# Two of four weight sums by adding transfers in the seven-product blocks of an MLP's down projection (Trainium2, one core)

## The chip, the core and the metric

The kernel runs on one core of one Trainium2 chip. Its time is the device time of one execution in microseconds, the median of several runs. Five engines work side by side, each from a queue of its own: PE (matrix products), DVE (element by element), ACT (element by element with a function; here mostly copies that round), POOL (a further element engine, which can also issue transfers) and SP (here transfers alone). Transfers are carried by 16 transfer engines, whichever queue has issued them.

## What is computed

One decoder layer over 256 tokens of width 2048 in float32: a norm, an input projection, two groups of attention heads, an output projection with a residual, and an MLP with a residual and a last norm. The change lies in the MLP's second product.

```python
def reference(x, ...):
    ...
    x = x + mixed @ w_out[l]                                        # (256, 2048) @ (2048, 2048)
    h = rms_norm(x, norm2_g[l])
    x = x + jnp.square(jax.nn.relu(h @ w_mlp_in[l])) @ w_mlp_out[l]  # 2048 -> 8192 -> 2048
    return rms_norm(x, final_norm_g)
```

## The kernel before

*Precision.* Every float32 operand is held as two rounded parts, hi and lo, with hi + lo the operand (lo is the residue after rounding). A product is then three matrix products: hi·hi, hi·lo, lo·hi. For weights, ACT makes hi from the loaded tile (whi from raw) and DVE subtracts to get lo (wlo). This "split" is done for 128 x 1024 weights at a time.

*The MLP.* It runs in four rounds of 2048 hidden units. In a round, 16 tiles of 128 rows by 512 columns form a column block; four column blocks of the up projection ("u") and four of the down projection ("d") follow one another. Weights are loaded in units of 512 rows by 512 columns (1 MB, tile raw, four tiles deep, `[128, 4, 512]`) by SP's queue, and are consumed in steps of two 128-row tiles. A raw tile can be loaded again when all that is read from it has been read; the function `load_more` keeps four units that aren't spent. A unit's last split marks it as spent.

*Seven products.* For seven of the 16 down blocks (d block 0 of the rounds 0 to 2, d block 1 of all rounds) a unit of 512 x 512 weights with its 256 tokens is regarded as a 2 x 2 matrix of blocks, tokens in two halves, rows in two halves (k tiles 0, 1 and 2, 3) and columns in two halves of 256. Instead of eight block products, seven are computed, from sums and differences of the activation blocks (mix_hi, mix_lo; made by `mix_activations`) and of the weight blocks. A unit has four steps: "near" (the lower weight rows as they are), "first" (the upper left block), "odd" (two weight sums) and "even" (two further ones). There are 28 such units. The weight sums are made on DVE: ahead of "near", one operation makes the tile both (128 x 1024) from differences of raw; it is split for "odd"; then two operations of 128 x 512 overwrite both with the sums for "even", and it is split again. With "odd", raw is spent. `drain_seven` adds the seven products, which stand in PSUM, into the residual xs with the right signs and the factor rstd2sq.

*Order.* A list of steps, written out when the program is built, sets the order on PE; "near", "first", "odd", a plain step, "even", then further plain steps. In the up blocks there is one unit to eight plain steps; where down block 1 is mixed with down block 2, a unit and two plain steps alternate, four times in a round (below: the alternating stretch). Splits are written several steps ahead of their products, as far as five rotating whi and wlo buffers allow, so an ACT split waits until PE has finished with an older buffer. Nothing reorders instructions.

Of the kernel before, what the change touches and what calls it, by code (L numbers as in the profile page):

```python
# [11 lines left out]
F32 = mybir.dt.float32  # L12
F32R = mybir.dt.float32r
BF16 = mybir.dt.bfloat16
AF = mybir.ActivationFunctionType
ALU = mybir.AluOpType
# [3 lines left out]
P = 128  # L20
D_MODEL = 2048
SEQ = 256
TB = SEQ // P
# [5 lines left out]
CW = 512  # L29
# [47 lines left out]
def kernel(  # L77
# [18 lines left out]
    nc = tc.nc  # L96
# [11 lines left out]
    few = ctx.enter_context(tc.tile_pool(name="few", bufs=1))  # L108
# [29 lines left out]
    steps = [(ci, s, "") for ci in range(mlp0) for s in range(chunks[ci][6] // 2)]  # L138
# [25 lines left out]
    raws, splits, spent = {}, {}, set()  # L164

    def load(i):
        if i >= len(steps) or steps[i][1] % 2 or (steps[i][0], steps[i][1] // 2) in raws:
            return
        ci, s, _ = steps[i]
        _, _, w, r0, c0, cols, _ = chunks[ci]  # L170
        t = wraw.tile([P, 4, CW + NH], F32, name="raw")
        src = w[r0 + s * 256:r0 + s * 256 + 512, c0:c0 + cols].rearrange("(k p) c -> p k c", p=P)
        raws[ci, s // 2] = t
        if i == 0:
            return t, src
        n = 2 if i == 2 else 4
        for k in range(0, 4, n):
            nc.sync.dma_start(t[:, k:k + n, :cols], src[:, k:k + n])

    def load_more():  # L180
        for ci, unit in units:
            if len(raws) - len(spent) >= 4:
                return
            if (ci, unit) not in raws:
                load(steps.index(next(p for p in steps if p[0] == ci and p[1] // 2 == unit)))
# [3 lines left out]
    def part_tiles(i, size, high, low):  # L189
        if i < mlp_start:  # L190
            pool, names = wsplit, ("whi", "wlo")
        else:
            ring[0] += 1
            pool, names = (late_tiles["ring"], ("whi5", "wlo5")) if ring[0] % 5 == 0 else (wsplit, ("whi", "wlo"))
        return [pool.tile([P, 2 * CW + LINE], F32R, name=n)[:, b:b + size] for n, b in zip(names, (high, low))]

    late_tiles, late_forms, sums_of = {}, ExitStack(), {}

    def halves(t):
        return t.rearrange("p k (f c) -> p f k c", f=2)  # L200

    def split_seven(i):
        ci, s, sub = steps[i]
        t = raws[ci, s // 2][:, :, :CW]
        half = CW // 2
        if sub == "near":
            both = sums_of[ci, s] = late_tiles["pool"].tile([P, 2, CW], F32, name="both")
            nc.vector.tensor_tensor(halves(both), t[:, :, half:].rearrange("p (f k) c -> p f k c", f=2),
                                    halves(t[:, :2]), op=ALU.subtract)
        if sub == "first":  # L210
            hi, lo = (late_tiles["pool"].tile([P, CW + LINE], F32R, name=n)[:, b:b + CW]
                      for n, b in (("fhi", NEAR), ("flo", NEAR)))
            src = t[:, :2, :half]
        else:
            hi, lo = part_tiles(i, 2 * CW, NEAR, NEAR)
            src = t[:, 2:] if sub == "near" else sums_of[ci, s]
        hi, lo = (a.rearrange("p (k c) -> p k c", k=2) for a in (hi, lo))
        splits[i] = (hi, lo)
        nc.scalar.activation(hi, src, AF.Copy)  # L219
        nc.vector.tensor_tensor(lo, src, hi.bitcast(F32), op=ALU.subtract)  # L220
        if sub == "odd":
            a, b = src[:, :, :half], src[:, :, half:]
            nc.vector.tensor_tensor(a, t[:, 2:, half:], a, op=ALU.subtract)
            nc.vector.tensor_tensor(b, t[:, 2:, :half], a, op=ALU.subtract)  # L224
            spent.add((ci, s // 2))

    def split(i, j0=0, n=2):
        if i >= len(steps):
# [46 lines left out]


    raw0, src0 = load(0)
    load_x(0, 2, nc.sync, slice(0, 1))
    load_row(0)
# [6 lines left out]
    load_row(1, nc.scalar)  # L286
    nc.scalar.dma_start(grow[0:16], norm1_g[0].rearrange("(k p) -> k p", p=P))
    load(2)
    for c in range(2, 4):
        load_x(4 * c, 4 * c + 4)  # L290
# [65 lines left out]
    def rsqrt(dst, ssq, n):  # L356

        w = dst.shape[1]
        v = few.tile([P, TB], F32, name="rs_v", bufs=2)[:, :w]
        t = few.tile([P, TB], F32, name="rs_t", bufs=2)[:, :w]  # L360
        nc.vector.tensor_scalar(v, ssq, 1.0 / n, EPS, op0=ALU.mult, op1=ALU.add)
        nc.gpsimd.tensor_tensor(dst, v, half_t[:, :w], op=ALU.pow)
        nc.vector.tensor_tensor(t, dst, dst, op=ALU.mult)
        nc.vector.tensor_tensor(t, t, v, op=ALU.mult)
        nc.vector.tensor_scalar(t, t, -0.5, 1.5, op0=ALU.mult, op1=ALU.add)
        nc.vector.tensor_tensor(dst, dst, t, op=ALU.mult)
# [349 lines left out]
    ssq2s = few.tile([P, TB], F32, name="ssq2s")  # L716
    rstd2 = few.tile([P, TB], F32, name="rstd2")
    rstd2sq = few.tile([P, TB], F32, name="rstd2sq")

    def drain_o(kind, c, ci):  # L720
        acc = accs.pop(ci)
        for t in range(TB):
            xc = xs[:, t, c * CW:(c + 1) * CW]
            nc.vector.scalar_tensor_tensor(xc, acc[t], rstdo[kind][:, t:t + 1], xc, op0=ALU.mult, op1=ALU.add)
            if kind == 1:
                unused = two.tile([P, CW], F32, name="nat")
                nc.scalar.activation(unused, xc, AF.Square, accum_out=ssq2[:, t, c:c + 1])

    def second_norm():
        nc.vector.tensor_reduce(ssq2s, ssq2, axis=mybir.AxisListType.X, op=ALU.add)  # L730
        rsqrt(rstd2, ssq2s, D_MODEL)
        nc.vector.tensor_tensor(rstd2sq, rstd2, rstd2, op=ALU.mult)

    def squares():
        return rows_at(big_hi, BIG_HI), rows_at(big_lo, BIG_LO)
# [19 lines left out]
    def mix_activations(c):  # L755

        a, b = kept[c]
        (a11, a21), (a12, a22) = ((x[:, :, :P], x[:, :, P:]) for x in (a, b))
        nc.vector.tensor_tensor(a22, a21, a22, op=ALU.add)
        nc.vector.tensor_tensor(a21, a11, a21, op=ALU.subtract)  # L760
        nc.vector.tensor_tensor(a11, a22, a11, op=ALU.subtract)  # L761
        nc.vector.tensor_tensor(a12, a12, a11, op=ALU.subtract)

    def split_mixed(c):
# [19 lines left out]
    def drain_seven(r, c, ci, part):  # L784
        one_, two_, three, four = accs[ci]
        half = CW // 2
        left, right = slice(0, half), slice(half, CW)

        def add(t, cs, acc):
            xc = xs[:, t, cs]  # L790
            if len(acc.shape) > 2:
                xc = xc.rearrange("p (f c) -> p f c", f=2)
            nc.vector.scalar_tensor_tensor(xc, acc, rstd2sq[:, t:t + 1], xc, op0=ALU.mult, op1=ALU.add)

        cs = slice(c * CW, (c + 1) * CW)
        rest = three[:, right]
        if part == 0:
            s = late_tiles["ring"].tile([P, 2, half], F32, name="copies")
            late_tiles["copies"] = s
            nc.scalar.activation(s[:, 0], three[:, left], AF.Copy)  # L800
            nc.scalar.activation(s[:, 1], four[:, left], AF.Copy)
            nc.vector.tensor_tensor(rest, rest, s[:, 0], op=ALU.add)
            add(0, cs, one_)
        elif part == 1:
            add(0, cs, three)
            add(0, slice(cs.start + half, cs.stop), two_[:, right])
        elif part == 2:
            nc.vector.tensor_tensor(rest, rest, late_tiles["copies"][:, 1], op=ALU.add)
            add(1, cs, two_)
        else:  # L810
            add(1, cs, rest[:, None, :].to_broadcast([P, 2, half]))
            accs.pop(ci)
        if r == ROUNDS - 1 and part % 2:
            square_and_gain(part // 2, cs, c)

    def square_and_gain(t, cs, n):
        unused = two.tile([P, CW], F32, name="nat")
        nc.scalar.activation(unused[:, :cs.stop - cs.start], xs[:, t, cs], AF.Square, accum_out=ssq3[:, t, n:n + 1])
        if n > 2:
            put_gain(t, cs)  # L820
# [213 lines left out]
```

## Time and profile before

| | |
|---|---|
| median of three runs | 1089.61 us (1089.52 to 1090.16) |
| profiled execution | 1087.94 us, of which 1086.2 us span of the trace |
| busy share of the span | PE 99%, PE's weight loads 93%, DVE 74%, ACT 56%, POOL 3% |
| granted PE clock | 0.997 |
| moved by transfers | 209.26 MB, 193 GB/s |

The span runs from the first instruction to the last; the rest of the execution's time lies around it. A busy share is that of an engine over the whole span. In rows of groups, a name such as wlo<-raw,whi gives the tiles written and read, x28 the count, then the busy time in us, the mean of one in ns, and the engine's idle time ahead of them with what ended it. Rows of the order of time begin with start and duration in us.

### The profile page before, as it was taken

Reading aid. Unit: us, or ns where it says so; the run is one execution under the profiler, and the core shown is the slowest. Engines: PE = TensorE matmul, PEld = TensorE weight load, DVE = VectorE, ACT = ScalarE, POOL = GpSimd, SP = SyncE. Lnnn points to the kernel's source line nnn. Section 1 sums busy time; section 2 is a strip of 40 time slices with the busy share of each in tenths; the row PEclk is TensorE's granted clock in tenths of the full one; section 3 lists DMA queues with packets and bytes.
Section 4 is the critical chain, followed back from the end, with each engine's and each line's share of the span. In section 5 each row is a group of like instructions: output and inputs, shape, how many; then the busy total and the mean of one; then the engine's idle time right before and its main releaser. Section 6 shows DMA issues by size and latency. Waiting matters only on the chain.

```text
span 1086.2 us, 18976 instructions
## 1 busy us (share of the span) xinstructions
PE 1073.9 (99%) x7877; PEld 1007.0 (93%) x7877; DVE 800.3 (74%) x1076; ACT 604.4 (56%) x821; POOL 28.0 (3%) x42
## 2 busy tenths in 40 slices
PE   8999999999999999999999999999999999999996
PEld 7999899998988899998999998899998999999886
DVE  6667756667577666568877788887778886778885
ACT  6555545545454555565546665556665545666561
POOL 0010200000001000000000000000000000000000
PEclk9999999999999999999999999999999999999998
DMA  9764564655545566655675655665656665656552
GB/s 322 237 228 161 157 199 149 194 165 181 199 155 185 164 184 210 193 190 192 203 215 193 203 197 171 208 203 174 204 204 210 187 195 187 195 195 232 193 195 78
DMA packets 105394, 209.26 MB, mean 193 GB/s; under 512 B 3971, under 2 KB 5084, under 8 KB 105180
## 3 DMA queue, kind: packets, MB, share of 16 engines
q1 hardware_dynamic: 104412, 206.59, 58.3%
q8 instruction: 61, 1.00, 0.4%
q0 software_dynamic: 304, 1.06, 0.3%
q10 hardware_dynamic: 592, 0.40, 0.2%
q14 instruction: 25, 0.20, 0.1%
HBM read 205.93 MB, written 2.11 MB: 192 GB/s over the span
## 4 chain that ended last, share of the span: by engine, by line
PE 99%; DMA 0%; DVE 0%; POOL 0%; ACTq 0%; DVEq 0%; issue 0%
PE acc L417 48%; PE acc L401 34%; PE sc L461 7%; PE tr L461 5%; PE tr L350 1%; PE sc L691 1%; PE sc L401 1%; PE sc L647 1%; PE tr L675 0%; DMA xs<-in_x_dram 0%; PE sc L643 0%; PE sc L693 0%; PE sc L637 0%; PE sc L641 0%; DVE xs L859 0%; PE sc L695 0%
## 5 line engine op out<-in xcount | busy, mean ns | idle before, releaser
L254 DVE TENSOR_TENSOR wlo<-raw,whi 128x1024 fp32r<-128x1024 f32 (+2 forms) x327 | 394.0, 1220 | 155.2 <-ACT whi L253 152.9
L253 ACT ACTIVATE whi<-raw 128x1024 fp32r<-128x1024 f32 (+2 forms) x328 | 339.3, 1050 | 223.5 <-PE acc L417 130.4
L417 PE MATMUL acc<-aT_hi,whi 128*128 128x256 f32 x1536 | 425.6, 277 | 0.0
L417 PE MATMUL acc<-aT_hi,wlo 128*128 128x256 f32 x1536 | 424.0, 276 | 0.0
L417 PE MATMUL acc<-aT_lo,whi 128*128 128x256 f32 x1536 | 423.8, 276 | 0.0
L417 PEld LDWEIGHTS acc<-aT_hi,whi 128*128 128x128 f32 x1536 | 288.2, 188 | 1.2 <-issue 0.9
L417 PEld LDWEIGHTS acc<-aT_lo,whi 128*128 128x128 f32 x1536 | 288.2, 188 | 0.3
L417 PEld LDWEIGHTS acc<-aT_hi,wlo 128*128 128x128 f32 x1536 | 288.1, 188 | 0.1
L401 PE MATMUL acc<-whi,big_lo 128*128 128x512 f32 (+1 forms) x414 | 160.8, 388 | 0.0
L401 PE MATMUL acc<-whi,big_hi 128*128 128x512 f32 (+1 forms) x414 | 160.3, 387 | 0.0
L401 PE MATMUL acc<-wlo,big_hi 128*128 128x512 f32 (+1 forms) x414 | 160.0, 386 | 0.0
L401 PEld LDWEIGHTS acc<-wlo,big_hi 128*128 128x128 f32 x414 | 77.8, 188 | 15.9
L401 PEld LDWEIGHTS acc<-whi,big_lo 128*128 128x128 f32 x414 | 77.7, 188 | 15.2
L401 PEld LDWEIGHTS acc<-whi,big_hi 128*128 128x128 f32 x414 | 77.7, 188 | 15.2
L219 ACT ACTIVATE whi<-both 128x1024 fp32r<-128x1024 f32 x56 | 59.7, 1067 | 52.6 <-DVE both L224 24.8
L220 DVE TENSOR_TENSOR wlo<-both,whi 128x1024 fp32r<-128x1024 f32 x56 | 68.3, 1220 | 7.5 <-ACT whi L219 6.5
L337 DVE TENSOR_TENSOR big_lo<-nat,big_hi 128x512 fp32r<-128x512 f32 x32 | 22.2, 693 | 43.7 <-ACT big_hi L336 43.7
L401 PE MATMUL acc<-whi,aT_hi 128*128 128x512 f32 (+1 forms) x144 | 51.7, 359 | 0.0
L401 PE MATMUL acc<-whi,aT_lo 128*128 128x512 f32 (+1 forms) x144 | 51.0, 354 | 0.0
L401 PE MATMUL acc<-wlo,aT_hi 128*128 128x512 f32 (+1 forms) x144 | 51.0, 354 | 0.0
L219 ACT ACTIVATE whi<-raw 128x1024 fp32r<-128x1024 f32 x28 | 29.6, 1058 | 11.8 <-PE acc L401 6.4
L336 ACT ACTIVATE mix_hi<-nat 128x512 fp32r<-128x512 f32 x32 | 18.5, 625 | 29.9 <-DVE nat L761 29.9
(212 smaller groups left out, 1351.2 us busy)
## 6 DMA issues: line engine op xcount, KB each, us to landing
raw<-in_w_mlp_in_dram SPq DMA_DIRECT2D x64, 1024.0 KB, 5.7
raw<-in_w_mlp_out_dram SPq DMA_DIRECT2D x64, 1024.0 KB, 5.1
raw<-in_w_in_dram SPq DMA_DIRECT2D x42, 1024.0 KB, 5.1
raw<-in_w_out_dram SPq DMA_DIRECT2D x16, 1024.0 KB, 5.0
raw<-in_w_in_dram SPq DMA_DIRECT2D x4, 1040.0 KB, 8.5
xs<-in_x_dram SPq DMA_DIRECT2D x3, 512.0 KB, 9.7
raw<-in_w_in_dram SPq DMA_DIRECT2D x2, 512.0 KB, 5.4
big_lo<-rel_d POOLq DMA_DIRECT2D x1, 1024.0 KB, 7.2
```

The lines of the kernel that those rows point to most:

```text
L219: nc.scalar.activation(hi, src, AF.Copy)
L220: nc.vector.tensor_tensor(lo, src, hi.bitcast(F32), op=ALU.subtract)
L253: nc.scalar.activation(hi[:, :, c:c + step], t[:, :, c:c + step], AF.Copy)
L254: nc.vector.tensor_tensor(lo, t, hi.bitcast(F32), op=ALU.subtract)
L336: nc.scalar.activation(hi, src, AF.Copy)
L337: nc.vector.tensor_tensor(lo, src, hi.bitcast(F32), op=ALU.subtract)
L350: nc.tensor.transpose(p[:, j * SEQ + t * P:j * SEQ + (t + 1) * P], xs[:, t, c:c + P], ident)
L401: nc.tensor.matmul(acc, x, part[:, j, cols], start=go and n == 0, stop=end and n == 2, skip_group_check=True)
L417: nc.tensor.matmul(acc, w[:, j, b * P:(b + 1) * P], a[:, kt, :], start=kt == 0 and b % 2 == 0 and n == 0, stop=kt == kts - 1 and n == 2, s ...
L461: nc.tensor.matmul(acc, a[:, k, tokens], w[:, j, n * half:(n + 1) * half], start=fresh and x == 0, stop=s == KT // 2 - 2 and j == 1 and x ...
L647: nc.tensor.matmul(s[:, c0:c1], q[:, a, h, rows], k[:, b, h, keys], start=False, stop=n == 2, skip_group_check=True)
L691: nc.tensor.matmul(y[:, :SEQ], v[:, 0, dims], p[:, m, :SEQ], start=n == 0, stop=False, skip_group_check=True)
```

## The change

Two of the four weight sums of a unit are no longer made by DVE from raw. One is made in place, by a transfer issued on POOL that adds the upper left block of the weights, read again from memory, to the upper right block in raw. The other goes into a new tile third (128 x 2 x 256, two buffers): SP's queue loads the upper right block into it, and POOL's queue adds the lower right block. "odd" is then split from raw's upper right part and from third, in two halves each on ACT and DVE. Two additions on DVE within raw follow, and "even" is split from raw, at once, in a four-dimensional form. With "even", and no longer with "odd", raw is spent. The signs of one block column are turned round: two subtractions become additions among the weights, and on the activations, the drain and its factor (rstd2neg) the signs follow; the last drain is done in two halves of 256 columns instead of one broadcast over 512.

```diff
@@ load
+        if steps[i][2]:
+            half = CW // 2
+            third = sums_of[ci, s] = late_tiles["pool"].tile([P, 2, half], F32, name="third", bufs=2)
+            nc.sync.dma_start(third, src[:, :2, half:])
+            nc.gpsimd.dma_start(t[:, :2, half:CW], src[:, :2, :half], accum_op=ALU.add)
+            nc.gpsimd.dma_start(third, src[:, 2:, half:], accum_op=ALU.add)
@@ split_seven
-        if sub == "near":
-            both = sums_of[ci, s] = late_tiles["pool"].tile([P, 2, CW], F32, name="both")
-            nc.vector.tensor_tensor(halves(both), t[:, :, half:].rearrange("p (f k) c -> p f k c", f=2),
-                                    halves(t[:, :2]), op=ALU.subtract)
...
-            src = t[:, 2:] if sub == "near" else sums_of[ci, s]
+            parts = {"near": [(slice(0, CW), t[:, 2:])],
+                     "odd": [(left, t[:, :2, right]), (right, sums_of.get((ci, s)))],
+                     "even": [(left, t[:, :2, right]), (right, t[:, 2:, right])]}[sub]
...
-        nc.scalar.activation(hi, src, AF.Copy)
-        nc.vector.tensor_tensor(lo, src, hi.bitcast(F32), op=ALU.subtract)
+        if sub == "even":
+            h, l = (a.rearrange("p k (f c) -> p f k c", f=2) for a in (hi, lo))
+            x = t[:, :, right].rearrange("p (f k) c -> p f k c", f=2)
+            nc.scalar.activation(h, x, AF.Copy)
+            nc.vector.tensor_tensor(l, x, h.bitcast(F32), op=ALU.subtract)
+            spent.add((ci, s // 2))
+            return
+        for c, x in parts:
+            nc.scalar.activation(hi[:, :, c], x, AF.Copy)
+            nc.vector.tensor_tensor(lo[:, :, c], x, hi[:, :, c].bitcast(F32), op=ALU.subtract)
         if sub == "odd":
-            a, b = src[:, :, :half], src[:, :, half:]
-            nc.vector.tensor_tensor(a, t[:, 2:, half:], a, op=ALU.subtract)
-            nc.vector.tensor_tensor(b, t[:, 2:, :half], a, op=ALU.subtract)
-            spent.add((ci, s // 2))
+            sums_of.pop((ci, s))
+            first, second = t[:, :2, right], t[:, 2:, right]
+            nc.vector.tensor_tensor(first, first, second, op=ALU.add)
+            nc.vector.tensor_tensor(second, first, t[:, 2:, left], op=ALU.add)
@@ second_norm
+        nc.vector.tensor_scalar(rstd2neg, rstd2sq, -1.0, None, op0=ALU.mult)
@@ mix_activations
-        nc.vector.tensor_tensor(a22, a21, a22, op=ALU.add)
+        nc.vector.tensor_tensor(a22, a21, a22, op=ALU.subtract)
         nc.vector.tensor_tensor(a21, a11, a21, op=ALU.subtract)
-        nc.vector.tensor_tensor(a11, a22, a11, op=ALU.subtract)
+        nc.vector.tensor_tensor(a11, a11, a22, op=ALU.subtract)
@@ drain_seven
-            nc.vector.tensor_tensor(rest, rest, s[:, 0], op=ALU.add)
+            nc.vector.tensor_tensor(rest, rest, s[:, 0], op=ALU.subtract)
...
-            nc.vector.tensor_tensor(rest, rest, late_tiles["copies"][:, 1], op=ALU.add)
+            nc.vector.tensor_tensor(rest, rest, late_tiles["copies"][:, 1], op=ALU.subtract)
...
-            add(1, cs, rest[:, None, :].to_broadcast([P, 2, half]))
+            add(1, slice(cs.start, cs.start + half), rest, rstd2neg)
+            add(1, slice(cs.start + half, cs.stop), rest)
```

On DVE, one period of the alternating stretch reads so before: the difference (both), the splits of "near", "first" and "odd", the two sums for "even", a plain split, "even", a plain split.

```order
L208 TENSOR_TENSOR both<-raw 128x2x2x256
L220 TENSOR_TENSOR wlo<-raw,whi 128x1024
L220 TENSOR_TENSOR flo<-raw,fhi 128x512
L220 TENSOR_TENSOR wlo<-both,whi 128x1024
L223 TENSOR_TENSOR both<-raw,both 128x2x256
L224 TENSOR_TENSOR both<-raw,both 128x2x256
L254 TENSOR_TENSOR wlo<-raw,whi 128x1024
L220 TENSOR_TENSOR wlo<-both,whi 128x1024
```

And the same period on DVE after the change:

```order
L230 TENSOR_TENSOR wlo<-raw,whi 128x1024
L230 TENSOR_TENSOR flo<-raw,fhi 128x512
L230 TENSOR_TENSOR wlo<-raw,whi 128x2x256
L230 TENSOR_TENSOR wlo<-third,whi 128x2x256
L234 TENSOR_TENSOR raw<-raw 128x2x256
L235 TENSOR_TENSOR raw<-raw 128x2x256
L264 TENSOR_TENSOR wlo<-raw,whi 128x1024
L225 TENSOR_TENSOR wlo<-raw,whi 128x2x2x256
```

The first row is gone, the split of "odd" stands in two rows, the sums are written into raw, and raw is read until the last row. On SP's queue the alternating stretch now has a transfer into third behind every unit's load (x2 stands for a unit's load and a plain unit's load):

```order
L182 DMA third<-in_w_mlp_out_dram 128x2x256
L178 DMA raw<-in_w_mlp_out_dram 128x4x512 x2
L182 DMA third<-in_w_mlp_out_dram 128x2x256
L178 DMA raw<-in_w_mlp_out_dram 128x4x512 x2
L182 DMA third<-in_w_mlp_out_dram 128x2x256
```

On POOL's queue, which has nothing between the MLP's start and the last norm before the change, stand two transfers for each unit, 56 in all. The one into raw waits for the unit's load, the one into third for the transfer on SP:

```order
L183 DMA raw<-in_w_mlp_out_dram 128x2x256
L184 DMA third<-in_w_mlp_out_dram 128x2x256
L183 DMA raw<-in_w_mlp_out_dram 128x2x256
L184 DMA third<-in_w_mlp_out_dram 128x2x256
L183 DMA raw<-in_w_mlp_out_dram 128x2x256
```

What moved there is where a sum is waited for: ACT's split of "odd" now waits for these transfers, the splits of "near" and "first" for the unit's load alone. PE's order of products has not moved.

More of the change, by code (lines that the diff above doesn't have):

```diff
@@ L197 @@
     late_tiles, late_forms, sums_of = {}, ExitStack(), {}
-    def halves(t):
-        return t.rearrange("p k (f c) -> p f k c", f=2)
     def split_seven(i):
@@ L205, in split_seven @@
         half = CW // 2
-        if sub == "near":
-            both = sums_of[ci, s] = late_tiles["pool"].tile([P, 2, CW], F32, name="both")
-            nc.vector.tensor_tensor(halves(both), t[:, :, half:].rearrange("p (f k) c -> p f k c", f=2),
-                                    halves(t[:, :2]), op=ALU.subtract)
+        left, right = slice(0, half), slice(half, CW)
         if sub == "first":
@@ L212, in split_seven @@
                       for n, b in (("fhi", NEAR), ("flo", NEAR)))
-            src = t[:, :2, :half]
+            parts = [(slice(0, half), t[:, :2, left])]
         else:
             hi, lo = part_tiles(i, 2 * CW, NEAR, NEAR)
-            src = t[:, 2:] if sub == "near" else sums_of[ci, s]
+            parts = {"near": [(slice(0, CW), t[:, 2:])],
+                     "odd": [(left, t[:, :2, right]), (right, sums_of.get((ci, s)))],
+                     "even": [(left, t[:, :2, right]), (right, t[:, 2:, right])]}[sub]
         hi, lo = (a.rearrange("p (k c) -> p k c", k=2) for a in (hi, lo))
         splits[i] = (hi, lo)
-        nc.scalar.activation(hi, src, AF.Copy)
-        nc.vector.tensor_tensor(lo, src, hi.bitcast(F32), op=ALU.subtract)
+        if sub == "even":
[8 more added lines that the diff above has]
+            nc.vector.tensor_tensor(lo[:, :, c], x, hi[:, :, c].bitcast(F32), op=ALU.subtract)
         if sub == "odd":
-            a, b = src[:, :, :half], src[:, :, half:]
-            nc.vector.tensor_tensor(a, t[:, 2:, half:], a, op=ALU.subtract)
-            nc.vector.tensor_tensor(b, t[:, 2:, :half], a, op=ALU.subtract)
-            spent.add((ci, s // 2))
+            sums_of.pop((ci, s))
+            first, second = t[:, :2, right], t[:, 2:, right]
+            nc.vector.tensor_tensor(first, first, second, op=ALU.add)
+            nc.vector.tensor_tensor(second, first, t[:, 2:, left], op=ALU.add)
     def split(i, j0=0, n=2):
@@ L718 @@
     rstd2sq = few.tile([P, TB], F32, name="rstd2sq")
+    rstd2neg = few.tile([P, TB], F32, name="rstd2neg")
     def drain_o(kind, c, ci):
@@ L787, in drain_seven, with add @@
         left, right = slice(0, half), slice(half, CW)
-        def add(t, cs, acc):
+        def add(t, cs, acc, scale=rstd2sq):
             xc = xs[:, t, cs]
-            if len(acc.shape) > 2:
-                xc = xc.rearrange("p (f c) -> p f c", f=2)
-            nc.vector.scalar_tensor_tensor(xc, acc, rstd2sq[:, t:t + 1], xc, op0=ALU.mult, op1=ALU.add)
+            nc.vector.scalar_tensor_tensor(xc, acc, scale[:, t:t + 1], xc, op0=ALU.mult, op1=ALU.add)
         cs = slice(c * CW, (c + 1) * CW)
```

## The prediction

> **What bounds the kernel now.** I read the page's busy table and its chain of waits first, then windows over the stage that the change touches, then that stage's order of time.
>
> ```profile
> span 1086.2 us, 18976 instructions
> PE 1073.9 (99%) x7877; PEld 1007.0 (93%) x7877; DVE 800.3 (74%) x1076; ACT 604.4 (56%) x821; POOL 28.0 (3%) x42
> PE 99%; DMA 0%; DVE 0%; POOL 0%; ACTq 0%; DVEq 0%; issue 0%
> ...
> 397.00:545.00 148.00, 148.00 (x1107) 139.63 (x1105) 105.27 (x123) 84.22 (x102) 0.69 (x1) 1.00 0.62 198
> 545.00:1086.00 541.00, 531.99 (x4034) 504.36 (x4032) 431.12 (x507) 306.87 (x368) 2.42 (x4) 0.99 0.59 192
> ```
>
> The last two rows are windows (length; busy of PE, PEld, DVE, ACT, POOL; granted clock; DMA share; GB/s). From 397 us, where the MLP begins, PE is busy for 680.0 of 689.0 us, and the missing 9.0 us lie at the very end, behind its last product. So what the change takes from DVE is not on the path, unless PE itself goes faster or begins to wait. The chain in order of time tells more (start, length, piece):
>
> ```profile
> 361.96 10.91 PE acc L401 x48
> ...
> 481.68 22.25 PE acc L401 x96
> 545.40 10.90 PE acc L417 x96
> ...
> 651.51 22.25 PE acc L401 x96
> ...
> 482.00:492.00 10.00, 10.00 (x45) 8.10 (x44) 7.51 (x11) 7.63 (x11) 0.00 (x0) 1.00 0.37 116
> ...
> 651.00:673.00 22.00, 22.00 (x99) 17.91 (x98) 18.11 (x24) 13.21 (x17) 0.00 (x0) 1.00 0.54 179
> ```
>
> A product of 512 columns takes 10.91/48 = 227 ns in the output projection and 22.25/96 = 232 ns in the down projection. If all 816 such products of the down projection with 512 columns (9 plain column blocks of 96, less the 48 of the last) ran at 227 ns, 816 x 4.5 ns = 3.7 us would be won. That is the largest reserve that I find on PE's stretch.
>
> **The change, term by term.**
>
> PE. The sequence of matrix products, their operands and shapes is the same row for row, so its own time changes by 0.
>
> DVE and ACT, per unit (28 units), from the groups kept apart by shape:
>
> ```profile
> L208 DVE TENSOR_TENSOR both<-raw 128x1024 f32<-128x1024 f32 x28 | 34.1, 1218 | 0.0
> L220 DVE TENSOR_TENSOR wlo<-both,whi 128x1024 fp32r<-128x1024 f32 x56 | 68.3, 1220 | 7.5 <-ACT whi L219 6.5
> L223 DVE TENSOR_TENSOR both<-raw,both 128x512 f32<-128x512 f32 x28 | 19.4, 692 | 1.0
> L220 DVE TENSOR_TENSOR flo<-raw,fhi 128x512 fp32r<-128x512 f32 x28 | 19.1, 684 | 0.0
> L219 ACT ACTIVATE whi<-both 128x1024 fp32r<-128x1024 f32 x56 | 59.7, 1067 | 52.6 <-DVE both L224 24.8 <-DVE both L208 12.8 <-PE acc L401 11.9
> L219 ACT ACTIVATE fhi<-raw 128x512 fp32r<-128x512 f32 x28 | 17.2, 616 | 0.0
> L793 DVE SCALAR_TENSOR_TENSOR xs<-sc,rstd2sq,xs 128x512 f32<-128x512 f32 x14 | 10.4, 741 | 0.0
> L793 DVE SCALAR_TENSOR_TENSOR xs<-sc,rstd2sq,xs 128x256 f32<-128x256 f32 x7 | 3.4, 484 | 0.2
> ```
>
> The subtraction into both goes: -28 x 1.218 = -34.1 us. The residue of the "odd" form is made in two halves: 28 x (2 x 0.684 - 1.220) = +4.1. The two additions that follow stand in for the two subtractions at 0.692 each: 0. The last drain is split: 7 x (2 x 0.484 - 0.741) = +1.6, and the other signs cost nothing more. DVE: -28.4 us, and one small negation ahead of the MLP. ACT: 28 x (2 x 0.616 - 1.067) = +4.6 us. All of it runs beside PE, so 0 on the path; if that cover were gone, the gain could be at most the 28.4 us.
>
> Loads. The source of every unit is now read 1.75 times: one more plain transfer on SP's queue and two that add at the destination on POOL's, 256 KB each. No transfer of before adds, so its cost has to be bounded. First, how long one may take. The rows are one unit's in the stretch in which units alternate with plain steps: SP's issues, DVE, ACT, and PE's first "odd" product and the plain product behind it.
>
> ```profile
> 506.14 0.37 SPq L178 DMA_DIRECT2D raw<-in_w_mlp_out_dram  x1
> 511.64 0.37 SPq L178 DMA_DIRECT2D raw<-in_w_mlp_out_dram  x1
> ...
> 508.90 1.22 DVE L220 TENSOR_TENSOR wlo<-both,whi 128x1024 fp32r<-128x1024 f32 x1
> 510.16 0.69 DVE L223 TENSOR_TENSOR both<-raw,both 128x512 f32<-128x512 f32 x1
> 510.89 0.69 DVE L224 TENSOR_TENSOR both<-raw,both 128x512 f32<-128x512 f32 x1
> 512.79 1.22 DVE L220 TENSOR_TENSOR wlo<-both,whi 128x1024 fp32r<-128x1024 f32 x1
> ...
> 507.47 1.07 ACT L219 ACTIVATE whi<-both 128x1024 fp32r<-128x1024 f32 x1 [0.46 <-PE tr L461]
> 520.38 1.06 ACT L253 ACTIVATE whi<-raw 128x1024 fp32r<-128x1024 f32 x1 [1.48 <-PE acc L401]
> 528.19 1.07 ACT L219 ACTIVATE whi<-both 128x1024 fp32r<-128x1024 f32 x1 [0.46 <-PE tr L461]
> ...
> 516.22 0.28 PE L461 MATMUL sc<-whi,mix_hi 128*128 128x256 f32 x1
> 517.58 0.39 PE L401 MATMUL acc<-whi,big_hi 128*128 128x512 f32 x1
> ```
>
> The load at 511.64 goes out when the last subtraction of the unit two before is done (510.89 + 0.69). In the changed kernel a raw buffer is read until the "even" residue is made, here at 512.79 + 1.22 = 514.0, about 0.4 sooner with DVE's shorter list: 513.6. The "odd" form of the unit so loaded begins on ACT at 528.19: 14.6 us later (it was 16.6). And PE does not need it then: for the unit ahead ACT began at 507.47 and PE at 516.22. Working back over what stands in between on DVE (plain residue 1.22, two additions 1.38, two residues 1.37, and ACT's first half 0.62, the sum 4.6, to be done when PE wants the plain step at 517.58), "odd" may begin at 513.0, so 5.5 us late. Limit from issue to sum: 14.6 without any lateness, 20.1 before PE waits.
>
> Second, how long it takes.
>
> ```profile
> raw<-in_w_mlp_out_dram SPq DMA_DIRECT2D x64, 1024.0 KB, 5.1
> big_lo<-rel_d POOLq DMA_DIRECT2D x1, 1024.0 KB, 7.2
> out_dram<-xs SPq DMA_DIRECT2D x4, 256.0 KB, 2.6
> rel_d<-neg POOLq DMA_DIRECT2D x1, 12.0 KB, 1.9
> ...
> 67.28 0.74 POOL L542 DMA_DIRECT2D rel_d<-neg  x1 [31.12 <-DVE neg L541]
> 69.49 0.98 POOL L545 DMA_DIRECT2D big_lo<-rel_d  x1 [1.47 <-DVE gate_s L528]
> 66.90 1.20 DVE L254 TENSOR_TENSOR wlo<-raw,whi 128x1024 fp32r<-128x1024 f32 x1
> ```
>
> Main load 5.1; POOL, which has no other work in the MLP, issues in about 1.0 each; an adding transfer of 256 KB lands in between 2.6 (a plain one of that size) and 7.2 (the 1 MB of POOL's queue, four times its bytes). Nearest is POOL's own queue: 1.9 fixed, (7.2 - 1.9)/4 = 1.3 for the bytes, taken twice because the destination is read too: 4.5. One behind the other: 5.1 + 2 x (1.0 + 4.5) = 16.1, with the second partly beside the first rather less. Ends: 5.1 + 2 x 3.6 = 12.3 and 5.1 + 2 x 8.2 = 21.5. So "odd" is 1.5 us late or less and PE has 4.0 us left. The added plain transfer sits on SP's queue, where it holds the next raw load up by one issue, 0.37 us; that load, out at 506.14 us, was read at 520.38, so it hides. On POOL the second transfer queues behind the first one's wait, which is counted; no other instruction of POOL is due before the end.
>
> The Trainium skill ("DMA: Bandwidth & Descriptors", Anatomy of one DMA — SWDGE (gpsimd) path) fits 2.0 us plus bytes over 436 GB/s, an estimate of 2.6 us for 256 KB; by it the way from issue to sum would be 12.3 us and the time the same. No run here yet shows an adding transfer.
>
> Third, the engines that carry it all.
>
> ```profile
> 506.00:516.36 10.36, 10.36 (x69) 9.31 (x68) 8.94 (x10) 5.85 (x7) 0.00 (x0) 1.00 0.62 204
> 548.00:574.50 26.50, 26.50 (x236) 26.50 (x235) 18.83 (x21) 13.71 (x16) 0.00 (x0) 1.00 0.65 199
> ```
>
> One period of the alternating stretch, 10.36 us, has 0.62 x 10.36 = 6.4 us of transfers for 2.1 MB. By bytes 0.75 MB more is +2.3; with the two adding ones counted double +3.8: 10.2, just under the period. If an adding transfer costs four times its bytes, 6.4 + 0.8 + 6.1 = 13.3, so 2.9 us short in each period. In the other stretch a unit has 26.5 us and room for all of these.
>
> The sum: PE 0, DVE and ACT 0, loads 0. The profiled execution took 1087.94 us (1086.2 of span); the median of the timed runs is 1089.61, 1.7 above it. I forecast no change against either: 1089.6.
>
> **Rivals.**
>
> *PE waits for the sums: slower.* If an adding transfer lands only over 6.5 us after its issue (5.1 + 2 x (1.0 + 6.5) = 20.1), the limit breaks in the alternating stretches, four of them with four units, of which the first two are loaded early. At the upper end of 21.5 each of the other two costs 1.4 us: 8 x 1.4 = +11, 1100.8. If instead the transfer engines run short by 2.9 a period, 4 x 2.9 - 5.5 = 6.1 us in each of the four stretches, +24: 1114. For it speaks that the reserve is a few us and the price unknown; against it that both bounds nearest to the work stay inside. Chance 0.22.
>
> *POOL's issue is held up by DVE: slower.* If DVE's SBUF operations kept POOL from writing out its transfers, an issue of 0.98 would last to a gap in DVE's work. With DVE busy for 8.9 of 10.36 us, two issues would take about 2 x 0.98 x 10.36/1.4 = 14.5 instead of 2.0 us, 28.6 from issue to sum, 8.5 over the limit; 8 units late: some +68, 1158. Against it: the issue of 0.74 us at 67.28 lies wholly under a DVE TENSOR_TENSOR from 66.90 to 68.10. The Trainium skill ("SBUF — State Buffer", Who interferes with whom) has DVE's two-port modes of copy and tensor_scalar block a DMA issued on POOL, and tensor_tensor not; the units' DVE work is tensor_tensor, and the overlap just shown agrees. Chance 0.03.
>
> *A lighter DVE lets PE run faster.* Were the 232 ns DVE's doing, up to 3.7 us would come back: 1085.9. Against it: the two stretches of 96 products last 22.25 us alike at a DVE share of 0.75 and 0.82 and of ACT at 0.76 and 0.60. Chance 0.05, with whatever else helps.
>
> **How the numbers follow.** No change: 0.70. A measurement of this kernel can tell about 0.2%, 2.2 us, from no change; the three runs differ by 0.6. Slower by more: 0.22 + 0.03 = 0.25; faster by more: 0.05. The likeliest case has 1087.4 to 1091.8 to itself. The range goes from 1087.6, which leaves out most of the faster case, to 1098, which takes in the mild forms of the first rival (up to 8 of its 11 to 24 us): 0.70 and some 0.10.
>
> **What the profile after would show.** Right: PE's order and its 680 us from the MLP's start the same, the 22.25 us stretches as before; DVE near 772 us and ACT near 609; both gone from the groups; 56 more issues on POOL of about 1 us, landing in 3 to 6 us; from 193 to about 213 GB/s. ACT's wait for the adding transfers, if any, 1 to 2 us per unit. Wrong: idle time of PE in the alternating stretches, ended by ACT or DVE's whi and wlo, with those waiting for third or raw; a DMA share near 1.0 there; POOL's issues of several us; or a pitch of the 512-column products other than 232 ns.

## The result, and the profile after

The change makes the kernel 0.7% slower: 1096.13 us (median of 4 runs, 1095.29 to 1097.18) against 1089.88 us (4 runs, 1089.52 to 1090.49), a ratio of 1.0069 with a 95% interval of 1.0057 to 1.0081. (The two medians alone are 6.25 us apart, a quotient of 1.0057, the lower end of that interval.) The forecast was no change, 1089.6; it is wrong by 6.5 us. The profiled execution took 1097.18 us, 9.2 more than that of before; 1.4 of this lies ahead of the MLP, whose start varies from 397.0 to 399.2 us among the profiled executions of this document.

The page after, its span, busy shares and transfers:

```profile
span 1095.4 us, 19234 instructions
PE 1084.1 (99%) x7877; PEld 1016.6 (93%) x7877; DVE 772.9 (71%) x1084; ACT 607.3 (55%) x849; POOL 96.3 (9%) x98
...
DMA packets 128244, 231.30 MB, mean 211 GB/s; under 512 B 5315, under 2 KB 27932, under 8 KB 128028
```

PE has as many products as before and is busy 10.2 us longer (1084.1 less 1073.9). All that it waits for, by the view of waits, lies ahead of the MLP:

```profile
PE tr L360 <- DMA xs<-in_x_dram: 1.2, 1, 1.2
PE sc L327 <- DVE relx L304: 1.2, 1, 1.2
```

So the time is not in a wait: the products themselves come slower. The chain in order of time (start, length, piece) shows where. Before, a few rows that the prediction did not show: the MLP's first 744 products, the start of two neighbouring units in an alternating stretch (514.33 and 524.68) and in an up block (582.83 and 609.35), and PE's last piece:

```profile
397.34 84.34 PE acc L417 x744
...
514.33 1.38 PE sc L461 x12
...
524.68 1.38 PE sc L461 x12
...
582.83 1.36 PE sc L461 x12
...
609.35 1.36 PE sc L461 x12
...
1059.83 17.18 PE acc L401 x123
```

The same pieces after:

```profile
398.73 84.98 PE acc L427 x744
483.71 22.28 PE acc L411 x96
...
516.53 1.42 PE sc L471 x12
...
527.06 1.42 PE sc L471 x12
...
586.02 1.42 PE sc L471 x12
...
613.02 1.42 PE sc L471 x12
...
1061.60 24.94 PE acc L411 x156
```

From the start of the 744 products to the end of the last piece, called PE's stretch below, it is 1077.01 - 397.34 = 679.67 us before and 1086.54 - 398.73 = 687.81 after: 8.1 us more. That is the slowdown. The 744 products of 256 columns take 0.64 us more. A unit with its plain steps takes 10.53 instead of 10.35 us in the alternating stretch (16 such units) and 27.00 instead of 26.52 among the up blocks (12 such). That makes 0.6 + 16 x 0.18 + 12 x 0.48 = 9.3, of which some overlaps or varies; adding up all starts in the trace gives 3.1 us in the up projection, 4.8 in the units' products and 0.3 in the plain down products. The 512-column products have kept their pitch (22.28 us for 96; before 22.25).

The 744 products belong to the first up blocks, and are done before any adding transfer lands. The order of time on PE shows what happens in them after the change (start, length; the length is modelled, so the distances between starts count):

```profile
404.37 0.28 PE L427 MATMUL acc<-aT_hi,whi 128*128 128x256 f32 x1
...
406.75 0.28 PE L427 MATMUL acc<-aT_hi,whi 128*128 128x256 f32 x1
...
409.58 0.28 PE L427 MATMUL acc<-aT_hi,whi 128*128 128x256 f32 x1
```

From 404.37 to 406.75 there are 21 products, 113.3 ns each. From 406.75 to 409.58 there are 24, one step of the list, 117.9 ns each; then 113 ns again. Every fifth step is slow like this: these are the steps whose weights stand in the fifth pair of the rotating buffers, whi5 and wlo5. Six such steps of 24 products, 4.5 ns longer each, are the 0.64 us.

The fifth pair is allotted when the MLP begins, behind the pool `few`. The change adds one tile to `few`, on a line that the prediction costed as "one small negation":

```
+    rstd2neg = few.tile([P, TB], F32, name="rstd2neg")
```

It holds 8 bytes per partition and is allotted 32. In the built program everything behind `few` therefore stands 32 bytes higher in SBUF: whi5, wlo5, third and the halves fhi, flo at 32 beyond a multiple of 256 (before at 0), mix_hi at 128 (before 96), mix_lo at 0 (before 224). The kernel sets these places with unused tiles (`late_begin`, and `late_hi`, `late_lo` of MIX_HI and MIX_LO words). What stands ahead of `few`'s end has not moved: the first four pairs of whi and wlo, aT_hi and aT_lo, big_hi and big_lo.

The adding transfers among POOL's groups (busy us, mean ns of one issue | idle time ahead and what ended it):

```profile
L184 POOL DMA_DIRECT2D third<-in_w_mlp_out_dram x28 | 46.3, 1653 | 1.0 <-DMA third<-in_w_mlp_out_dram 0.7 <-issue 0.3
L183 POOL DMA_DIRECT2D raw<-in_w_mlp_out_dram x28 | 33.8, 1206 | 567.6 <-DMA raw<-in_w_mlp_out_dram 240.6 <-DMA third<-in_w_mlp_out_dram 98.9 <-DVE wlo L264 77.9
```

And in the table of issues (KB each, median us from issue to landing):

```profile
raw<-in_w_mlp_out_dram POOLq DMA_DIRECT2D x28, 256.0 KB, 6.1
third<-in_w_mlp_out_dram POOLq DMA_DIRECT2D x28, 256.0 KB, 6.7
```

### The profile page after: what moved, and what is told of

The parts are those of the page before. It is cut to its first block, busy times and chain, and to the rows that moved or that the text cites. A ratio compares the mean times of both kernels' runs of the same rounds, so it can differ in the third digit from the quotient of the medians.

```text
span 1095.4 us, 19234 instructions
## 1 busy us (share of the span) xinstructions
PE 1084.1 (99%) x7877; PEld 1016.6 (93%) x7877; DVE 772.9 (71%) x1084; ACT 607.3 (55%) x849; POOL 96.3 (9%) x98
## 4 chain that ended last, share of the span: by engine, by line
PE 99%; DMA 0%; DVE 0%; POOL 0%; ACTq 0%; DVEq 0%; issue 0%
PE acc L427 48%; PE acc L411 34%; PE sc L471 7%; PE tr L471 5%; PE tr L360 1%; PE sc L701 1%; PE sc L411 1%; PE sc L657 1%; PE tr L685 0%; DMA xs<-in_x_dram 0%; PE sc L653 0%; PE sc L703 0%; PE sc L647 0%; PE sc L651 0%; PE sc L327 0%; DVE xs L870 0%
## 5 line engine op out<-in xcount | busy, mean ns | idle before, releaser
L263 ACT ACTIVATE whi<-raw 128x1024 fp32r<-128x1024 f32 (+2 forms) x328 | 340.2, 1050 | 235.3 <-PE acc L427 129.4
L183 POOL DMA_DIRECT2D raw<-in_w_mlp_out_dram x28 | 33.8, 1206 | 567.6 <-DMA raw<-in_w_mlp_out_dram 240.6
L229 ACT ACTIVATE whi<-raw 128x1024 fp32r<-128x1024 f32 (+1 forms) x56 | 47.2, 842 | 28.3 <-PE acc L411 6.1
L230 DVE TENSOR_TENSOR wlo<-raw,whi 128x1024 fp32r<-128x1024 f32 (+1 forms) x56 | 53.4, 954 | 8.3 <-ACT whi L229 8.3
L184 POOL DMA_DIRECT2D third<-in_w_mlp_out_dram x28 | 46.3, 1653 | 1.0 <-DMA third<-in_w_mlp_out_dram 0.7
```

Source lines behind the costliest of these rows:

```text
L183: nc.gpsimd.dma_start(t[:, :2, half:CW], src[:, :2, :half], accum_op=ALU.add)
L184: nc.gpsimd.dma_start(third, src[:, 2:, half:], accum_op=ALU.add)
L229: nc.scalar.activation(hi[:, :, c], x, AF.Copy)
L230: nc.vector.tensor_tensor(lo[:, :, c], x, hi[:, :, c].bitcast(F32), op=ALU.subtract)
L263: nc.scalar.activation(hi[:, :, c:c + step], t[:, :, c:c + step], AF.Copy)
```

## The experiments

Times are medians on one chip per group of runs, with the kernel before on the same chip beside them; that had medians of 1087.70 us beside e1 to e4, 1088.61 beside e5 to e8 and 1088.11 beside e9 and e10. The ratios and 95% intervals are those on record, and can differ from the quotient of two medians by up to 0.0012. PE's stretch is taken from the chain's two rows as above.

| kernel | median, us | ratio to before | PE's stretch, us |
|---|---|---|---|
| before | | | 679.67 |
| after | 1096.13 | 1.0069 (1.0057 to 1.0081) | 687.81 |
| e1: before, and one tile more | 1095.32 | 1.0071 (1.0059 to 1.0083) | 687.80 |
| e2: after, without the tile | 1088.98 | 1.0011 (0.9997 to 1.0025) | 684.28, with PE's waits of 3.5 |
| e3: before, mix tiles 32 bytes on | 1092.39 | 1.0039 (1.0027 to 1.0051) | 684.43 |
| e4: before, weight tiles 32 bytes on | 1092.86 | 1.0046 (1.0034 to 1.0058) | 685.39 |
| e5: before, all 64 bytes on | 1095.81 | 1.0070 (1.0056 to 1.0084) | 688.09 |
| e6: before, all 128 bytes on | 1091.55 | 1.0029 (1.0020 to 1.0038) | 682.28 |
| e7: e2 with one adding transfer a unit | 1089.04 | 1.0005 (0.9996 to 1.0014) | 679.66 |
| e8: before, squares moved | 1089.50 | 1.0004 (0.9995 to 1.0013) | 680.24 |
| e9: before, plain down weights 64 bytes on | 1088.66 | 1.0004 (0.9995 to 1.0013) | 679.78 |
| e10: before, plain down weights 192 bytes on | 1090.85 | 1.0021 (1.0012 to 1.0030) | 681.81 |

Three theories stood at the start. PLACE: where the tiles stand in SBUF sets the pitch of the products, and the new tile moved them. TRANSFERS: the adding transfers and the larger traffic slow PE's reads. ORDER: the moved splits and sums on DVE and ACT do.

**e1, the kernel before with one unused tile of the same size in `few`.**

```
+    spare = few.tile([P, TB], F32, name="spare")
+    nc.gpsimd.memset(spare, 0.0)
```

> The kernel before with one more tile of 128 x 2 float32 in the pool few, at the place where rstd2neg stands in the changed kernel, and nothing else of the change. In the build it takes 32 bytes per partition, so that whi5, wlo5, copies, mix_hi, mix_lo, both, fhi and flo move up by 32 bytes. Theory PLACE (the slower products come from where these tiles stand in SBUF): the same pitch of 118 instead of 113 ns on every fifth step of the up projection and in the units, PE's stretch 8 us longer, time about 1096 (+6 to +8). Theory TRANSFERS (the added traffic or the adding transfers slow PE's reads) and theory ORDER (other waits or signs do): no transfer, wait or sign differs, so 1089.9.

The chain of e1, its first up blocks and PE's last piece:

```profile
397.05 84.98 PE acc L417 x744
...
1059.91 24.94 PE acc L401 x156
```

The tile alone, with no adding transfer and no moved step, makes the kernel before 0.71% slower, and both pieces last as long as after the change, to the last digit. TRANSFERS and ORDER have nothing left to explain in the median.

**e2, the changed kernel with the negated factor in an older tile** (ssq2s, which is no longer read by then), so that everything stands where it stood before.

```
-    rstd2neg = few.tile([P, TB], F32, name="rstd2neg")
+    rstd2neg = ssq2s
```

> The changed kernel, whole, but rstd2neg is written into the tile ssq2s, which is no longer read by then, so that no tile is added and whi5, wlo5, mix_hi, mix_lo, fhi and flo stand where they stood before (third where both stood). PLACE: 1089.9, within 2 us, pitch 113 ns again, the forecast of no change holds for the rest of the change. TRANSFERS or ORDER: 1096 as the changed kernel.

The slowdown is gone: 1.0011, with 1 inside the interval. The twelve runs scatter, though: nine lie from 1087.4 to 1089.9 us, and three at 1092.1, 1093.4 and 1095.4. The profiled run is the one of 1092.1. Its chain, the same two pieces and the first 96 plain down products:

```profile
397.18 84.34 PE acc L427 x744
481.53 22.25 PE acc L411 x96
...
1069.35 12.11 PE acc L411 x100
```

Its waits of PE, the rows from the MLP (us in total, times, longest):

```profile
PE tr L471 <- ACT whi L263: 1.3, 1, 1.3
...
PE acc L411 <- ACT whi L263: 1.3, 1, 1.3
...
PE acc L411 <- DVE wlo L264: 0.5, 1, 0.5
PE sc L471 <- DVE xs L803: 0.4, 1, 0.4
```

PE in order of time around the first of them:

```profile
898.67 0.28 PE L471 MATMUL sc<-whi,mix_lo 128*128 128x256 f32 x1
900.28 0.36 PE L471 MATMUL tr<-whi,mix_hi 128*128 128x256 f32 x1 [1.33 <-ACT whi L263]
```

ACT in order of time, the "odd" split of a unit ahead of it, with the idle time before each row and what ended it:

```profile
891.49 0.63 ACT L229 ACTIVATE whi<-raw 128x512 fp32r<-128x512 f32 x1 [4.93 <-DMA raw<-in_w_mlp_out_dram]
894.53 0.63 ACT L229 ACTIVATE whi<-third 128x512 fp32r<-128x512 f32 x1 [2.40 <-DMA third<-in_w_mlp_out_dram]
```

DVE in order of time: its second residue of "odd", and the last drain of the block of units before:

```profile
895.19 0.69 DVE L230 TENSOR_TENSOR wlo<-third,whi 128x512 fp32r<-128x512 f32 x1 [2.34 <-ACT whi L229]
...
899.65 0.48 DVE L803 SCALAR_TENSOR_TENSOR xs<-tr,rstd2sq,xs 128x256 f32<-128x256 f32 x1
```

The adding transfers of e2 in the table of issues:

```profile
raw<-in_w_mlp_out_dram POOLq DMA_DIRECT2D x28, 256.0 KB, 6.7
third<-in_w_mlp_out_dram POOLq DMA_DIRECT2D x28, 256.0 KB, 7.9
```

The 84.34 us of before are back. But in one unit ACT waits 4.93 us for the sum in raw and 2.40 for the one in third, DVE's residues wait for ACT, and the drains that stand behind them on DVE are late by that. PE stands still from 898.67 to 900.28: its next products write the PSUM tile tr that the last of these drains reads, and go on when it is done (899.65 + 0.48 = 900.13). The split named in the bracket (whi, L263) writes a tile that these products do not read. A second stop of about the same length follows at 1066.4, behind a late split on ACT; 20 us ahead of it ACT has waited 5.65 us for the last unit's sum in third, but the way from there to the stop is not shown. So the first rival of the prediction is seen in one unit of one run, and perhaps in a second.

**e3 and e4, the two halves of the shift.** e3 moves mix_hi and mix_lo by 32 bytes (both, fhi and flo, which follow them, by 256) and leaves whi5 and wlo5; e4 moves whi5, wlo5 and the tiles both, fhi and flo, and leaves the mix tiles.

```
e3: -MIX_HI, MIX_LO = 24, 32
    +MIX_HI, MIX_LO = 32, 32
e4: +MIX_HI, MIX_LO = 16, 32
    -            late5.tile([P, 24], F32R, name="late_begin")
    +            late5.tile([P, 32], F32R, name="late_begin")
```

> The kernel before with mix_hi and mix_lo alone moved up by 32 bytes (a spacer of 32 instead of 24 words; both, fhi and flo move by 256 bytes, whi5 and wlo5 not at all). PLACE: slower only in the units' products, whose operands these are: 24 of 42 products of each of 28 units read them, at 5 ns that is +3.4 us, up to +4.8 if the products in between are slowed too; the up projection stays at 113 ns. TRANSFERS or ORDER: 1089.9.

> The kernel before with whi5, wlo5, both, fhi and flo moved up by 32 bytes, mix_hi and mix_lo where they were (spacers of 32 and 16 instead of 24 and 24 words). PLACE: every fifth step of the up projection at 118 ns, +2.6 to +3.1 us, and of the units those products that read fhi, flo or whi5: together +3 to +5. With the kernel in which mix alone moved it adds up to the +6 to +8 of the added tile. TRANSFERS or ORDER: 1089.9.

The chain of e3:

```profile
397.00 84.34 PE acc L417 x744
...
514.15 1.42 PE sc L461 x12
...
524.70 1.42 PE sc L461 x12
...
1059.85 21.58 PE acc L401 x142
```

And of e4:

```profile
396.97 84.98 PE acc L417 x744
...
1059.96 22.40 PE acc L401 x145
```

In e3 the up projection is as before, and the period of a unit is 10.55 us as after. In e4 the up projection is as after. So the place counts for the operand that the kernel loads into the array: for whi5 in the up projection, where the activations pass, and for the mix tiles in the units, where the weights pass. It counts for the passing operand as well: the tiles that e4 moves pass in the units, and all starts added up give 2.9 us more there, beside 2.7 in the up projection. And a product is slowed by more than its own operands: in e3, 504 of the units' 1176 products read only tiles whose place within 256 bytes is that of before, and they make 1.5 of the units' 4.7 us. The two parts add 4.8 and 5.7 us to the stretch, 10.5 together, where the whole shift adds 8.1. They don't add up; whether the other operand or the products beside it make the difference is not separated here.

**e5 and e6, how far the place matters.** All the late tiles are moved by 64 or by 128 bytes. PLACE-64 takes the place within 64 bytes to count, so that both cost nothing; PLACE-256 the place within 256.

```
e5: +            late5.tile([P, 40], F32R, name="late_begin")
e6: +            late5.tile([P, 56], F32R, name="late_begin")
```

> The kernel before with all tiles of the pools late5 and late (whi5, wlo5, copies, mix_hi, mix_lo, both, fhi, flo) moved up by 64 bytes instead of 32. Theory PLACE-64 (what counts is the place within 64 bytes): as before, 1087.7 to 1089.9, all pitches at 113 ns. Theory PLACE-256 (the place within 256 bytes): slower by some us, like the added tile's +7.6, or in part of the products. TRANSFERS and ORDER: no change.

> The kernel before with the same tiles moved up by 128 bytes. PLACE-64: as before. If 64 bytes are slow and 128 are not, the period is 128; if both are slow, 256 or more. TRANSFERS and ORDER: no change.

The chain of e5:

```profile
397.40 85.14 PE acc L417 x744
...
1060.59 24.90 PE acc L401 x156
```

And of e6:

```profile
399.19 84.34 PE acc L417 x744
...
1059.81 21.66 PE acc L401 x142
```

By these rows e5's stretch is 8.4 us longer than before's: PLACE-64 falls. The stretch of e6 is 2.6 us longer: at 128 bytes the up projection is as quick as at 0, and the units' products are not. So the pattern does not repeat within 128 bytes. Whether it does within 256 is open: no run moves all of the tiles by 256.

**e7, one adding transfer a unit instead of two,** to tell whether e2's scatter comes from sums that land late (LATE) or is none of the change's (NOISE). third holds the upper right block and gets the upper left added; the other sum is made by one DVE operation of 128 x 512.

```
-            nc.gpsimd.dma_start(t[:, :2, half:CW], src[:, :2, :half], accum_op=ALU.add)
-            nc.gpsimd.dma_start(third, src[:, 2:, half:], accum_op=ALU.add)
+            nc.gpsimd.dma_start(third, src[:, :2, :half], accum_op=ALU.add)
+        if sub == "near":
+            nc.vector.tensor_tensor(t[:, :2, right], t[:, :2, right], t[:, 2:, right], op=ALU.add)
```

> The changed kernel with all tiles in their old places (rstd2neg in ssq2s), and with one adding transfer per unit instead of two: third gets the upper right block and the upper left one is added to it, while the other sum is made on DVE by one more addition of 128 x 512 in raw ahead of the near form. Same result. Theory LATE (what scatter and idle PE time is left with the tiles back in place comes from sums that land late, two adding transfers one behind the other): no idle time of PE over 1 us, spread of the runs as before's, ratio to before 1.000. Rival NOISE (the scatter has another cause): spread to 1095 as with two adding transfers, ratio 1.001. By either, no gain: DVE gets some 9 us lighter than before and PE stays the bound.

The chain of e7:

```profile
398.78 84.34 PE acc L428 x744
...
1059.88 18.56 PE acc L412 x129
```

And its adding transfers in the table of issues:

```profile
third<-in_w_mlp_out_dram POOLq DMA_DIRECT2D x28, 256.0 KB, 4.7
```

The eleven runs lie from 1087.25 to 1090.0, as closely as before's 26 (1087.14 to 1089.32), PE waits for nothing in the MLP, and its stretch is that of before. This bears LATE out, with three of e2's twelve runs against none of eleven here, and one trace of each. It brings no gain either: less work on DVE is worth nothing here.

**e8, e9 and e10, whether a better place can be had.** The 232 ns of the plain down products, which the prediction called the largest reserve, might be a matter of place too. e8 moves the squared activations to 32 within 256 bytes (before 96 and 224); e9 and e10 move the plain down weights instead, to 96 and to 224 (before 32). RELATION takes the distance between the two operands to count, STATIONARY the place of the activations alone.

```
e8:  +        return rows_at(big_hi, BIG_HI - 16), rows_at(big_lo, 0)
e9:  +            high, low = ... (HIGH, HIGH) if what == "d" else ...
e10: +            high, low = ... (LOW, LOW) if what == "d" else ...
```

> The kernel before with the squared activations (tiles big_hi and big_lo as the down projection reads them) at another place within their tiles: 32 and 32 bytes within 256, as the output projection reads the same tiles, instead of 96 and 224. PLACE: the down projection's products of 512 columns take 227 instead of 232 ns, -3.7 us; the units' products that read big_hi and big_lo may get slower by up to 5 ns, 588 of them, +2.9. So -3.7 to 0, and pitches that differ from before's. If place has nothing to do with the 232 ns: 0 in both groups.

> The kernel before with the weight parts of the plain down projection (whi and wlo there, the streamed operand of the 512-column products) 96 bytes into their line of 256 instead of 32; big_hi and big_lo stay at 96 and 224. Theory RELATION (the pitch follows the distance between the two operands' places; the output projection with both at 32 has 227 ns): products of whi and wlo with big_hi drop to 227 ns, -1.5 us, those with big_lo stay or change; total -3.7 to +2. Theory STATIONARY (only the place of the operand that is loaded as weights counts): no change of the 232 ns. If it wins, it is a version faster than both kernels.

> The same at 224 bytes. RELATION: the products with big_lo drop to 227 ns, -2 us, those with big_hi stay or change. STATIONARY: no change.

The chain of e8: the first 96 plain down products, and six products of a unit (0.68 us in before's units):

```profile
481.61 21.78 PE acc L401 x96
...
674.84 0.72 PE tr L461 x6
```

The same 96 products in the chain of e9:

```profile
481.33 22.19 PE acc L401 x96
```

And in that of e10, with PE's last piece:

```profile
483.32 22.39 PE acc L401 x96
...
1059.99 20.80 PE acc L401 x137
```

In e8 the pitch of the 512-column products falls to 21.78/96 = 226.9 ns, that of the output projection: the 232 ns were the place, and not DVE's doing. But those of the units' products that read the same activations (504, not the 588 of the expectation) rise from 113 to about 119 ns. By the starts added up the plain products win 2.7 us and the units lose 3.1, and the time is the same. e9 wins 0.06 us in 96 products, which the time does not show. e10 loses 0.14 there and 2.1 us in the whole stretch, 0.21% in the time; 0.6 of this is in the units, none of whose operands has moved: all of it in the 16 of the alternating stretches, which stand beside the plain down products, and 0.0 in the 12 among the up blocks. So what slows one group of products reaches into the next. Neither theory's numbers came. The weights' place does count, against STATIONARY. Against RELATION, in e9 the products of wlo with big_hi fall from 231 to 227 ns (median from start to start) as it says, but those of whi with big_hi, with the same places within 256 bytes, rise from 229 to 232. What rule sets the pitch stays open. No kernel here beats before.

## Why the prediction was wrong

**The step that failed** is the first term: "The sequence of matrix products, their operands and shapes is the same row for row, so its own time changes by 0." The rows are the same; the addresses are not. The term measured +8.1 us, and e1 shows that the tile alone makes it. The order of instructions names tiles and not where they stand, so the comparison on which the term rested could not show this. The cue was in the profile all the same: 227 against 232 ns for the same shape was seen and called a reserve, and DVE was the only cause for it that was weighed; and in the code, which sets places by tiles that nothing reads. Of the prediction's signs, "its 680 us from the MLP's start the same" failed (687.8), and so, by less, did "landing in 3 to 6 us" (6.1 and 6.7); the pitch that it watched, of the 512-column products, has hardly moved, and that of the 256-column products, which did, was not among the signs.

**The rest of the sum held in the median.** With the tile taken out (e2) the same change gives 1.0011, with no change inside the interval, though three of its twelve runs come later. DVE came to 772.9 us (forecast near 772), ACT to 607.3 (609), the transfers to 211 GB/s (213).

**The adding transfers were mis-sized.** Forecast were an issue of about 1.0 us and a landing of 4.5. The landings measured 6.1 and 6.7 (in e2's late run 6.7 and 7.9). A pair of issues took POOL 2.4 us: its busy time rose from 28.0 to 96.3 over 28 pairs, and the row of 1.65 overlaps the end of the one of 1.21. Put wholly one behind the other with the main load's 5.5 (e2 6.2), the landings, which count from the start of the issue, make 18.3 us in the changed kernel and 20.8 in e2, where PE's limit was 20.1. In the trace the second is mostly issued 0.7 us after the first, so the two run side by side, most units are in time, and a few are not. The limit itself was worked back from a plain split; the stop that was followed back came by DVE's drains. The estimate of 2.6 us from the Trainium skill ("DMA: Bandwidth & Descriptors", Anatomy of one DMA — SWDGE (gpsimd) path) is less than half of what these transfers took; by it there would be no scatter in e2.

**The rivals.** *PE waits for the sums* is a mechanism that does occur, with too high a price: not 11 to 24 us, but in the profiled run of e2 3.5 us of waits in all, in two stops for the most part; the median is within the bound. The changed kernel itself shows no wait of PE. Its result lies on the side of this rival for another reason. *POOL's issue is held up by DVE* falls: no issue takes several us, and the longest group has a mean of 1.65. *A lighter DVE lets PE run faster* falls twice: 22.25 us for 96 products in e2, where DVE's list is the shorter one and the tiles stand as before, and 21.78 in e8 by place alone. No rival stood for a change of the products' own pitch, so the time lies within the range by luck, for a reason that is not among those the range was made from.

## What to carry to other kernels

Where PE is the bound, a tile added anywhere can change the time of every product whose operands are allotted behind it: compare the addresses of the operands before and after, and not only the order of instructions. Here shifts of 32, 64 and 128 bytes all made a difference. Test a change that adds a tile against the kernel before with that tile alone; here that kernel takes 8 us off the change's account. And if two groups of products of one shape differ by 2% in pitch, ask first where their operands stand.

## What the runs showed of the hardware

- The pitch of products depends on where their operands stand in SBUF (the on-chip memory that holds the tiles), with nothing else changed: 113.3 or 117.9 ns for 256 columns (after), 226.9 (e8) or 231.8 ns (before) for 512, at a granted clock of 0.997 in each. Moving the late tiles by 32 or 64 bytes made the whole 0.7% slower (e1, e5), by 128 bytes 0.3% (e6). Products beside the slowed ones are slowed too (1.5 us in e3, 0.6 in e10). The Trainium skill ("SBUF — State Buffer", Operand start alignment) asks of an operand's start only that it be a multiple of the element size, and says that this is about legality and not speed; these runs put a number on the speed.
- A tile of 8 bytes per partition took 32, and moved all that was allotted behind it by as much (after, e1).
- A transfer of 256 KB that adds at its destination landed 4.7 us after its issue with one to a unit (e7), and 6.1 to 7.9 with two (after, e2); a pair of issues kept POOL busy for 2.4 us.
